# First feed-forward block with paired up tiles, and S5 set-up products on GpSimd

## The chip, the cores and the metric

The kernel runs on one core of a Trainium2 chip. The metric is the device time of one execution in microseconds, the median of the runs shown. Inside a core TensorE (PE in the profile) multiplies matrices into PSUM, VectorE (DVE) and ScalarE (ACT) work element by element, GpSimd (POOL) does so too and also issues some DMAs, and SyncE (SP) issues most DMAs. Each engine takes its instructions in the order in which they were written and waits for the others by semaphores.

## The reference, cut to what matters

The model is two blocks over 512 tokens of width 1024. The first block is a half-weighted SwiGLU feed-forward (the "first FFN", with weights w1, w3 of 1024 x 2816 and w2 of 2816 x 1024), a mixer made of an S5 state-space branch and a gated linear attention branch, and a second SwiGLU (the "second FFN") of the same shape. The second block is another mixer and a gated feed-forward with short convolutions.

```python
h = h + 0.5 * swiglu(rms_norm(h, ffn1_norm), ffn1_w1, ffn1_w3, ffn1_w2)   # (silu(x@w1) * (x@w3)) @ w2
u = rms_norm(h, mix_norm)
...                                                        # u @ w_in, S5 mixer, GLA mixer, w_out
h = h + 0.5 * swiglu(rms_norm(h, ffn2_norm), ffn2_w1, ffn2_w3, ffn2_w2)
# S5 mixer, the part that hangs on weights alone:
mag = exp(lam_re*dt); ar = mag*cos(lam_im*dt); ai = mag*sin(lam_im*dt)
bbar_re = fr*b_re - fi*b_im;  bbar_im = fr*b_im + fi*b_re  # and these times powers of (ar, ai)
```

## The kernel before

Activations lie transposed, as tiles of 128 features x 512 tokens; `KD` = 8 such tiles make the width, `NFF` = 22 make the hidden width. Every fp32 factor is split in two parts in the fp32r type, high (`wh`, `hgh`, `gh`) and low (`wl`, `hgl`, `gl`), and each product is three matmuls: high by high, high by low, low by high (`mm3`). ScalarE makes the high part by a copy and VectorE the low part by a subtraction (`wsplit`, `split_of`, `split`). For some weights (`moved=True`) the low part is made otherwise: ScalarE writes the negated high part, and a DMA issued by GpSimd adds the raw weight onto it (`dma_add`, L421); in the first FFN these are the w3 tiles.

No loop exists at run time: Python writes all operations into a `Recorder`, with an engine, a cost, a class (URGENT before MAIN before BACK) and the tiles they read and write. `Recorder.schedule` plays a planner through them with these costs, and the order that it finds on each engine is written out as the fixed instruction order. Tiles of 512 columns all come from one pool, `gen`, of 67 buffers; raw weights have 3 buffers (`raw`), split weights 4 each (`wh`, `wl`), combinations of weights 2 (`ws`). PSUM has 4 banks for the main products (`mm`) and 4 for side work (`aux`).

The first FFN: the up products of tiles 0 and 1 (`up0`) are worked out during the first loads. Tiles 2 to 21 follow one by one in `up_tile`: w1 and w3 products by `linear` (24 matmuls of 512 columns each), then the gate. The down product of tiles 0 to 15 goes through `gated`, `Pairs.put` and `down_pair`: four tiles make a part, and for two output tiles at a time `seven` computes a 2x2 block product by seven products of half width (256 tokens) in place of eight, with combinations of the weights (`ws`) and of the activations (`x1`, `x2`, `xa`, `xb`) made on VectorE. Tiles 16 to 21 go down plainly. `swiglu` calls `gated` and then does this plain rest.

The second FFN is `swiglu_pairs`: tiles 0 to 5 plainly by `up_tile`, tiles 6 to 21 two at a time by `pair8`, which forms the up product of two tiles by the same seven half-width products (7 x 4 x 3 = 84 matmuls of 256 columns for w1, and as many for w3), with combinations of the activations made once in `forms` and those of the weights in `ws`; the down products are plain, in five parts (`DOWN`), two output tiles per `linear_pair`.

`s5_prep` works out what the S5 branch needs of its weights. It is in class BACK and is planned into the first FFN's time: a chain on columns of 16 (tiles `sp`), then four blocks `b`, each with the cosines and sines (`ta`, `tt`, of 512 columns), the complex products of B and C with powers of the state matrix (elements of 128 columns, into `binr`, `bini`, `car`, `cai`, with `y1`, `y2` in an `sp` tile between), four transposes each and small matmuls on TensorE (`aux`), and spills to DRAM that GpSimd issues (`dram<-sw`, `dram<-T`). `s5_run` loads these again in the mixer.

All VectorE tensor-by-tensor operations have line L355, the scalar-tensor-tensor ones L367; all matmuls but transposes have L408.

Of the kernel before, what the change touches and what calls it, by code (L numbers as in the profile page):

```python
# [12 lines left out]
ALU = mybir.AluOpType  # L13
# [3 lines left out]
KD = D // 128  # L17
# [276 lines left out]
def body(ctx, tc, A, out):  # L294
    nc = tc.nc
# [55 lines left out]
    def dve1(o):  # L351
        return 0.068 + _size(o) / 960.0

    def tt(o, a, b, op):
        R.op("dve", dve1(o), lambda: nc.vector.tensor_tensor(out=o, in0=a, in1=b, op=op), [o], [a, b])  # L355

    def mul(o, a, b):
        tt(o, a, b, ALU.mult)

    def add(o, a, b):  # L360
        tt(o, a, b, ALU.add)
# [476 lines left out]
    UP0 = 6  # L838
    DOWN = ((0, 4), (4, 8), (8, 12), (12, 16), (16, NFF))

    def swiglu_pairs(hg, rB, h, done):
        a, jobs = [], []

        def down(p, n):
            k0, k1 = DOWN[p]
            for i, ps in enumerate(linear_pair("ffn2_w2_%d" % p, n, a[k0:k1])):
                add(h[n + i], ps, h[n + i])

        def queue():
            p = [k1 for _, k1 in DOWN].index(len(a)) if len(a) in [k1 for _, k1 in DOWN[:-1]] else None  # L850
            if p is not None:
                jobs.extend((p, n) for n in range(0, KD, 2))

        xs = forms(hg, [rB])
        for n in range(UP0):
            a.append(split(up_tile("ffn2_w1", "ffn2_w3", n, hg, rB), "g"))
            queue()
            if jobs:
                down(*jobs.pop(0))
        for i in range((NFF - UP0) // 2):  # L860
            us = pair8(A["ffn2_w1_g"][i], xs, rB)
            for u in us:
                act(u, u, AF.Silu)
            if jobs:
                down(*jobs.pop(0))
            vs = pair8(A["ffn2_w3_g"][i], xs, rB)
            for u, v in zip(us, vs):
                stt(v, v, 0.5, u, ALU.mult, ALU.mult)
                a.append(split(v, "g"))
            if jobs:  # L870
                down(*jobs.pop(0))
            queue()
        while jobs:
            down(*jobs.pop(0))
        p = len(DOWN) - 1
        for n in range(KD):
            ps = linear("ffn2_w2_%d" % p, n, a[DOWN[p][0]:])
            with cls(URGENT):
                add(h[n], ps, h[n])
                done(h[n], n)  # L880

    def swiglu(w1, w3, w2, hg, rB, h, done, up0=()):
        rest = gated(w2, lambda n: up_tile(w1, w3, n, hg, rB, up0), h)
        for n in range(KD):
            ps = linear(w2 + "_r", n, rest)
            with cls(URGENT):
                add(h[n], ps, h[n])
                done(h[n], n)
# [3 lines left out]
    with cls(BACK):  # L892
        s5_prep(locals())
    hg0, hg, st = hg, [None] * KD, []
    swiglu("ffn1_w1", "ffn1_w3", "ffn1_w2", hg0, rB, h,
           lambda t, n: norm_tile(t, Vall("mix_norm"), n, st, hg), up0)
    rB, rc = norm_end(st)
    h, hg, st = mixer1(locals())
    rB, _ = norm_end(st)
# [8 lines left out]
        norm_tile(t, fgm, n, st, hg)  # L908
        accumulate(st2, t, fg[:, n:n + 1])

    swiglu_pairs(hg0, rB, h, both)
    with cls(URGENT):
        r3 = rsqrt(mean_sq(1.0 / D, EPS, st[0]), 4)
        m2 = mean_sq(1.0 / D, 0.0, st2[0])
# [65 lines left out]
def s5_prep(env):  # L980
# [72 lines left out]
    def cmul(xr, xi, ar, ai, br, bi, t1, t2):  # L1053
# [4 lines left out]
        mul(t2, ai, br)  # L1058
        add(xi, t1, t2)

    t1, t2 = col(), col()
    P = {m: (col(), col()) for m in (1, 2, 3, 4)}
    mul(P[1][0], mag, cs)
# [35 lines left out]
    for b in range(4):  # L1099
        js = slice(4 * b, 4 * b + 4)  # L1100

        def bc(c, n):
            return c[:, js].unsqueeze(2).to_broadcast([128, 4, n])

        def spill(t):
            d = e.dtile(t.dtype)
            e.dma("pool", d, t)
            return d

        def copied(src):  # L1110
            t = lslot("sw")
            act(t if len(src.shape) == 2 else v3(t), src, AF.Copy)
            return spill(t)

        def v3(t):
            return t.rearrange("p (j c) -> p j c", j=4)


        A_, B_, n_, t_ = lslot("ta"), lslot("tb"), lslot("tn"), lslot("tt")
        io = e.Cc("iota").unsqueeze(1).to_broadcast([128, 4, 128])  # L1120
        mul(v3(A_), io, bc(ra, 128))
        mul(v3(B_), io, bc(rb, 128))
        add(n_, A_, B_)
        ts(n_, n_, INV2PI, MAGIC, ALU.mult, ALU.add)
        ts(n_, n_, MAGIC, None, ALU.subtract)
        stt(t_, n_, -C1, A_, ALU.mult, ALU.add)
        stt(t_, n_, -C23, t_, ALU.mult, ALU.add)
        add(t_, t_, B_)
        ts(t_, t_, -PI_SAFE, PI_SAFE, ALU.max, ALU.min)
        stt(A_, t_, -1.0, t_, ALU.mult, ALU.max)  # L1130
        act(t_, t_, AF.Sin)
        act(A_, A_, AF.Sin, scale=-1.0, bias=e.kbias[:, 1:2])
        d_cos, d_sin = spill(A_), spill(t_)


        B0 = lslot("b0")
        e.dma("sp", B0.rearrange("p (a j c) -> p a j c", a=4, j=4), e.A["s5bc"][:, :, js, :], after=[e.rB])
        b4 = B0.rearrange("p (a j c) -> p a j c", a=4, j=4)
        bre, bim, cre, cim = (b4[:, i] for i in range(4))
        bin_ = [lslot("binr"), lslot("bini")]  # L1140
        bv = [t.rearrange("p (j q c) -> p j q c", j=4, q=4) for t in bin_]
        y1 = x1.rearrange("p (j c) -> p j c", j=4)
        y2 = x2.rearrange("p (j c) -> p j c", j=4)
        cmul(bv[0][:, :, 3], bv[1][:, :, 3], bc(fr, 32), bc(fi, 32), bre, bim, y1, y2)
        for m in (1, 2, 3):
            cmul(bv[0][:, :, 3 - m], bv[1][:, :, 3 - m], bc(P[m][0], 32), bc(P[m][1], 32),
                 bv[0][:, :, 3], bv[1][:, :, 3], y1, y2)
        wr, wi = e.wide("car"), e.wide("cai")
        cr = wr.rearrange("p (j q c) -> p j q c", j=4, q=5)
        ci = wi.rearrange("p (j q c) -> p j q c", j=4, q=5)  # L1150
        e.vcopy(cr[:, :, 0], cre)
        ts(ci[:, :, 0], cim, -1.0, None, ALU.mult)
        for m in (1, 2, 3, 4):
            pr, pi = bc(P[m][0], 32), bc(P[m][1], 32)
            mul(y1, pr, cre)
            mul(y2, pi, cim)
            sub(cr[:, :, m], y1, y2)
            mul(y1, pr, cim)
            mul(y2, pi, cre)
            stt(ci[:, :, m], y1, -1.0, y2, ALU.mult, ALU.subtract)  # L1160
        d_cr, d_ci = (copied(t[:, :, 1:5].rearrange("p j q c -> p j (q c)")) for t in (cr, ci))

        d_bin = []
        for t in bin_:
            ps = e.auxps()
            for j in range(4):
                e.tr(ps[:, j * 128:(j + 1) * 128], t[:, j * 128:(j + 1) * 128])
            d_bin.append(copied(ps))


        ps = e.auxps()
        bb = [e.wide_u()[:, 0:512], e.wide_u()[:, 0:512]]
        for i in range(2):
            act(bb[i].rearrange("p (j q c) -> p j q c", j=4, q=4),
                bv[i][:, :, 3:4].to_broadcast([128, 4, 4, 32]), AF.Copy)
        for j in range(4):
            o = ps[:, j * 128:(j + 1) * 128]
            e.mm(o, bb[0][:, j * 128:(j + 1) * 128], wr[:, j * 160:j * 160 + 128], True, False)
            e.mm(o, bb[1][:, j * 128:(j + 1) * 128], wi[:, j * 160:j * 160 + 128], False, True)
        T = lslot("T")  # L1180
        e.zero(T, after=[ps])
        Tv = T.rearrange("p (j c) -> p j c", j=4)
        pv = ps.rearrange("p (j c) -> p j c", j=4)
        dIv = x3.rearrange("p (j c) -> p j c", j=4)
        mul(dIv, e.V("s5_d", 4 * b, 4).unsqueeze(2).to_broadcast([128, 4, 32]),
            e.Cc("i32").unsqueeze(1).to_broadcast([128, 4, 32]))
        for q in range(4):
            pr = slice(32 * q, 32 * q + 32)
            act(Tv[pr, :, 32 * q:128], pv[pr, :, 0:128 - 32 * q], AF.Copy)
            add(Tv[pr, :, 32 * q:32 * q + 32], Tv[pr, :, 32 * q:32 * q + 32], dIv[pr])  # L1190
        d_T = spill(T)
        e.s5w.append((d_bin[0], d_bin[1], d_cr, d_ci, d_T, d_cos, d_sin))
# [518 lines left out]
def arrays_of(inputs):  # L1711
    a = {k: np.asarray(v) for k, v in inputs.items()}
    r = {}
    r["x"] = np.ascontiguousarray(a["x"][0].T).reshape(8, 128, 512)
    for n in ("ffn2_w1", "ffn2_w3"):
        r[n] = _wlay(a[n][0][:, :768])
        r[n + "_g"] = _wpairs(a[n][0][:, 768:], ((0, 8),))
    for p in range(5):
        r["ffn2_w2_%d" % p] = _wlay(a["ffn2_w2"][0][512 * p:512 * p + 512 if p < 4 else None])
    for n in ("ffn1_w1", "ffn1_w3", "s5_glu_w",  # L1720
              "proj_s5", "proj_gla", "w_out", "w_in_2", "p_a_2", "p_b_2", "w_out_2", "w_up_2"):
        r[n] = _wlay(a[n][0])
    for n in ("ffn1_w2", "w_down_2"):
        r[n + "_s"] = _wpairs(a[n][0], ((0, 4), (4, 8), (8, 12), (12, 16)))
        r[n + "_r"] = _wlay(a[n][0][2048:])
    w = a["w_in"][0]
# [74 lines left out]
```

## Time and profile before

| what | value |
|---|---|
| time, median of 3 runs (lowest to highest) | 1780.22 us (1780.22 to 1780.59) |
| the profiled execution's own time | 1779.6 us |
| its span, first to last instruction | 1777.8 us |
| PE, DVE, ACT, POOL busy | 99%, 80%, 52%, 5% of the span |
| granted TensorE clock, mean | 0.997 |
| first FFN after its early tiles, first matmul of tile 2 to first of the mixer | 30.2 to 372.9 us |
| second FFN, first to last matmul | 692.7 to 1040.6 us |

The profiled execution lies 0.6 us under the median of the runs; 1.8 us of its time lie outside the span. A busy PE is not PE at its peak, since matmuls overlap and their ends are modelled: the spacing of matmul starts tells what one costs.

### The profile page before, as it was taken

The page shows a single profiled execution, that of the slowest core. Times are in us where ns is not written, and L with a number is a line of the kernel's source. Part 1 is how long each engine was busy: PE and PEld are TensorE (multiplying, and loading weights), DVE is VectorE, ACT ScalarE, POOL GpSimd, SP SyncE. Part 2 cuts the span into 40 slices and gives each one's busy share as a digit, 9 for nine tenths or more (in the row PEclk, how much of TensorE's full clock was granted, in tenths as well). Part 3 has the DMA queues.
Part 4 walks back from the last instruction along what each step waited for, and adds up shares of the span by engine and source line. Part 5 has one row for each costly group of instructions (what it writes and reads, how often), then busy time and mean ns, then how long its engine had stood idle before and what let it go on. Part 6 is the DMA issues. An engine that isn't in the chain of part 4 may idle for free. (4 is left out here: it accounts for less than half of the span.)

```text
span 1777.8 us, 25154 instructions
## 1 busy us (share of the span) xinstructions
PE 1760.8 (99%) x9514; PEld 1525.4 (86%) x9514; DVE 1422.5 (80%) x2604; ACT 929.0 (52%) x1263; POOL 96.1 (5%) x180
## 2 busy tenths in 40 slices
PE   9999999999999999999999999999999999999997
PEld 7888888878789888899999988888888888888886
DVE  8899999668799777678888889787856587887875
ACT  6444444432746533334444544999953454544443
POOL 0011111211100000000000001000000000000000
PEclk9999999999999999999999999999999999999998
DMA  8455455665313342322333334222234444444551
GB/s 247 118 151 164 141 159 169 180 222 179 104 48 107 108 142 83 107 83 96 109 105 106 97 113 165 84 95 95 81 104 142 119 119 141 121 130 135 138 142 48
DMA packets 77690, 222.17 MB, mean 125 GB/s; under 512 B 8736, under 2 KB 17728, under 8 KB 77568
## 3 DMA queue, kind: packets, MB, share of 16 engines
q1 hardware_dynamic: 64352, 175.68, 30.4%
q0 software_dynamic: 13072, 44.87, 10.5%
q8 instruction: 75, 1.23, 0.3%
q14 instruction: 47, 0.39, 0.1%
q10 hardware_dynamic: 144, 0.00, 0.0%
HBM read 182.77 MB, written 15.73 MB: 112 GB/s over the span
## 5 line engine op out<-in xcount | busy, mean ns | idle before, releaser
L408 PE MATMUL mm<-hgh,wh 128*128 128x512 f32 (+1 forms) x1440 | 539.2, 374 | 0.5 <-DVE ua L355 0.5
L408 PE MATMUL mm<-hgl,wh 128*128 128x512 f32 (+1 forms) x1440 | 539.1, 374 | 0.0
L400 ACT ACTIVATE wh<-raw 128x1024 fp32r<-128x1024 f32 (+3 forms) x315 | 304.1, 974 | 446.6 <-PE mm L408 314.2
L408 PE MATMUL mm<-hgh,wl 128*128 128x512 f32 (+1 forms) x1432 | 535.9, 374 | 0.0
L355 DVE TENSOR_TENSOR wl<-raw,wh 128x1024 fp32r<-128x1024 f32 (+3 forms) x272 | 298.9, 1100 | 43.4 <-ACT wh L400 42.5
L408 PEld LDWEIGHTS mm<-hgh,wh 128*128 128x128 f32 x1440 | 271.2, 188 | 45.2 <-DVE ua L355 0.9
L408 PEld LDWEIGHTS mm<-hgl,wh 128*128 128x128 f32 x1440 | 271.0, 188 | 44.0 <-issue 0.2
L408 PEld LDWEIGHTS mm<-hgh,wl 128*128 128x128 f32 x1432 | 270.2, 189 | 44.8 <-issue 0.2
L400 ACT ACTIVATE wh<-ws 128x1024 fp32r<-128x1024 f32 x76 | 80.6, 1061 | 134.6 <-PE mm L408 120.0
L355 DVE TENSOR_TENSOR h<-mm,h 128x512 f32<-128x512 f32 (+1 forms) x134 | 75.1, 560 | 56.2 <-PE mm L408 54.9
L408 PE MATMUL mm<-gl,wh 128*128 128x512 f32 x260 | 101.3, 390 | 0.0
L408 PE MATMUL mm<-gh,wl 128*128 128x512 f32 x260 | 101.2, 389 | 0.0
L408 PE MATMUL mm<-gh,wh 128*128 128x512 f32 x260 | 100.7, 390 | 0.0
L355 DVE TENSOR_TENSOR wl<-ws,wh 128x1024 fp32r<-128x1024 f32 x76 | 92.7, 1219 | 8.0 <-ACT wh L400 7.8
L408 PE MATMUL mm<-x1h,wl 128*128 128x256 f32 x304 | 86.1, 283 | 0.0
L408 PE MATMUL mm<-x1l,wh 128*128 128x256 f32 x304 | 86.1, 283 | 0.0
L408 PE MATMUL mm<-x1h,wh 128*128 128x256 f32 x304 | 86.0, 283 | 0.0
L408 PE MATMUL mm<-x2l,wh 128*128 128x256 f32 x304 | 85.6, 285 | 0.0
L408 PE MATMUL mm<-x2h,wl 128*128 128x256 f32 x304 | 84.2, 285 | 0.0
L408 PE MATMUL mm<-x2h,wh 128*128 128x256 f32 x304 | 84.0, 284 | 0.0
L400 ACT ACT_TABLE_LOAD x57 | 73.1, 1283 | 5.0 <-DMA yf<-dram 2.9
L367 DVE SCALAR_TENSOR_TENSOR y<-t,vec,y 128x511 f32<-128x511 f32 x88 | 65.7, 746 | 7.8 <-ACT y L400 6.9
(380 smaller groups left out, 3453.3 us busy)
## 6 DMA issues: line engine op xcount, KB each, us to landing
raw<-in_ffn_w_dram SPq DMA_DIRECT2D x68, 512.0 KB, 3.7
raw<-in_w_in_dram SPq DMA_DIRECT2D x50, 512.0 KB, 3.5
raw<-in_w_up_dram SPq DMA_DIRECT2D x44, 512.0 KB, 3.7
wl<-raw POOLq DMA_DIRECT2D x42, 512.0 KB, 4.5
raw<-in_ffn_w_g_dram SPq DMA_DIRECT2D x32, 512.0 KB, 3.8
raw<-in_ffn_w_s_dram SPq DMA_DIRECT2D x16, 512.0 KB, 4.5
raw<-in_w_out_dram SPq DMA_DIRECT2D x16, 512.0 KB, 3.5
raw<-in_w_down_s_dram SPq DMA_DIRECT2D x16, 512.0 KB, 4.8
```

What stands on the lines that cost most here:

```text
L355: R.op("dve", dve1(o), lambda: nc.vector.tensor_tensor(out=o, in0=a, in1=b, op=op), [o], [a, b])
L367: R.op("dve", dve1(o) + 0.06 * len(_aps(s)), lambda: nc.vector.scalar_tensor_tensor(out=o, in0=a, scalar=s, in1=b, op0=op0, op1=op1), [o], ...
L400: R.op("act", c, lambda: nc.scalar.activation(o, i, f, **kw), [o], _aps(i, scale, bias), table=TABLES.get(f), cls=cls, after=after)
L408: R.op("pe", c, lambda: nc.tensor.matmul(ps, a, b, start=start, stop=stop, **kw), [ps], [a, b])
```

## The change

The first FFN takes the second FFN's form. `swiglu_pairs` gets the name of the FFN (`f`) and the early tiles (`up0`) as arguments and is called for both; `swiglu` is gone, and `gated` with `seven` is left to the last feed-forward alone. So tiles 6 to 21 of the first FFN's up products go through `pair8`, all its down products become plain ones in five parts, and its w3 tiles 6 to 21 have their low parts made by VectorE. In both FFNs `forms` is called ahead of tile 2 in place of ahead of tile 0. Of `s5_prep`, the complex products of the four blocks are issued to GpSimd in place of VectorE: 24 operations for B and 20 for C in each block, on 128 columns; the four scalar-tensor-tensor operations of C in each block stay on VectorE.

```diff
+    def tt_pool(o, a, b, op):
+        R.op("pool", 0.1 + _size(o) / 480.0, lambda: nc.gpsimd.tensor_tensor(out=o, in0=a, in1=b, op=op), [o], [a, b])
...
-    def swiglu_pairs(hg, rB, h, done):
+    def swiglu_pairs(f, hg, rB, h, done, up0=()):
...
-        xs = forms(hg, [rB])
         for n in range(UP0):
-            a.append(split(up_tile("ffn2_w1", "ffn2_w3", n, hg, rB), "g"))
+            if n == 2:
+                xs = forms(hg, [rB])
+            a.append(split(up_tile(f + "_w1", f + "_w3", n, hg, rB, up0), "g"))
...
-            us = pair8(A["ffn2_w1_g"][i], xs, rB)
+            us = pair8(A[f + "_w1_g"][i], xs, rB)
...
-            vs = pair8(A["ffn2_w3_g"][i], xs, rB)
+            vs = pair8(A[f + "_w3_g"][i], xs, rB)
...
-    def swiglu(w1, w3, w2, hg, rB, h, done, up0=()):
-        rest = gated(w2, lambda n: up_tile(w1, w3, n, hg, rB, up0), h)
-        for n in range(KD):
-            ps = linear(w2 + "_r", n, rest)
-            with cls(URGENT):
-                add(h[n], ps, h[n])
-                done(h[n], n)
...
-    swiglu("ffn1_w1", "ffn1_w3", "ffn1_w2", hg0, rB, h,
-           lambda t, n: norm_tile(t, Vall("mix_norm"), n, st, hg), up0)
+    swiglu_pairs("ffn1", hg0, rB, h, lambda t, n: norm_tile(t, Vall("mix_norm"), n, st, hg), up0)
...
+    def cmul_p(xr, xi, ar, ai, br, bi, t1, t2):
+        e.tt_pool(t1, ar, br, ALU.mult)
+        e.tt_pool(t2, ai, bi, ALU.mult)
+        e.tt_pool(xr, t1, t2, ALU.subtract)
+        e.tt_pool(t1, ar, bi, ALU.mult)
+        e.tt_pool(t2, ai, br, ALU.mult)
+        e.tt_pool(xi, t1, t2, ALU.add)
...
-        cmul(bv[0][:, :, 3], bv[1][:, :, 3], bc(fr, 32), bc(fi, 32), bre, bim, y1, y2)
+        cmul_p(bv[0][:, :, 3], bv[1][:, :, 3], bc(fr, 32), bc(fi, 32), bre, bim, y1, y2)
         for m in (1, 2, 3):
-            cmul(bv[0][:, :, 3 - m], bv[1][:, :, 3 - m], bc(P[m][0], 32), bc(P[m][1], 32),
+            cmul_p(bv[0][:, :, 3 - m], bv[1][:, :, 3 - m], bc(P[m][0], 32), bc(P[m][1], 32),
                  bv[0][:, :, 3], bv[1][:, :, 3], y1, y2)
...
-            mul(y1, pr, cre)
-            mul(y2, pi, cim)
-            sub(cr[:, :, m], y1, y2)
-            mul(y1, pr, cim)
-            mul(y2, pi, cre)
+            e.tt_pool(y1, pr, cre, ALU.mult)
+            e.tt_pool(y2, pi, cim, ALU.mult)
+            e.tt_pool(cr[:, :, m], y1, y2, ALU.subtract)
+            e.tt_pool(y1, pr, cim, ALU.mult)
+            e.tt_pool(y2, pi, cre, ALU.mult)
             stt(ci[:, :, m], y1, -1.0, y2, ALU.mult, ALU.subtract)
```

The host lays out ffn1_w1, ffn1_w3 and ffn1_w2 as it did those of the second FFN.

## Rows read from the trace of the kernel before

**Rows 1.** The page, busy time of each engine over the span.
```profile
PE 1760.8 (99%) x9514; PEld 1525.4 (86%) x9514; DVE 1422.5 (80%) x2604; ACT 929.0 (52%) x1263; POOL 96.1 (5%) x180
```

**Rows 2.** Busy time by stretch: first FFN, second FFN.
```profile
core 0: us, PE busy (x) PEld busy (x) DVE busy (x) ACT busy (x) POOL busy (x), PEclk, DMA share, GB/s
30.20:372.90 342.70, 342.68 (x1872) 297.78 (x1873) 301.50 (x718) 162.92 (x227) 43.58 (x75) 1.00 0.53 156
692.70:1040.60 347.90, 347.90 (x2173) 315.64 (x2172) 282.48 (x418) 159.86 (x225) 0.00 (x0) 1.00 0.31 99
```

**Rows 3.** PE in order of time (start, us): ends of two gapless runs.
```profile
679.74 0.39 PE L408 MATMUL mm<-mgh,wh 128*128 128x512 f32 x1
...
692.66 0.39 PE L408 MATMUL mm<-hgh,wh 128*128 128x512 f32 x1
...
863.48 0.28 PE L408 MATMUL mm<-x1h,wh 128*128 128x256 f32 x1
...
866.36 0.28 PE L408 MATMUL mm<-x2h,wh 128*128 128x256 f32 x1
```

**Rows 4.** PE groups by shape in the first FFN: S5's small matmuls.
```profile
L408 PE MATMUL aux<-cai,wu 128*128 128x128 f32 x32 | 6.1, 273 | 0.0
```

**Rows 5.** Two stretches with `pair8` or half-width work, columns as Rows 2.
```profile
500.00:600.00 100.00, 100.00 (x721) 94.42 (x720) 95.14 (x199) 58.67 (x93) 1.05 (x2) 1.00 0.28 87
800.00:900.00 100.00, 100.00 (x707) 94.25 (x706) 87.18 (x127) 47.14 (x67) 0.00 (x0) 1.00 0.31 100
```

**Rows 6.** DVE groups by shape, second FFN (busy us, mean ns, idle before).
```profile
L355 DVE TENSOR_TENSOR wl<-raw,wh 128x1024 fp32r<-128x1024 f32 x44 | 53.7, 1220 | 5.4 <-ACT wh L400 5.2
...
L355 DVE TENSOR_TENSOR h<-mm,h 128x512 f32<-128x512 f32 x40 | 27.5, 687 | 13.8 <-PE mm L408 13.3
...
L355 DVE TENSOR_TENSOR ssum<-ssum,sq 128x512 f32<-128x512 f32 x13 | 8.4, 684 | 0.0
```

**Rows 7.** Busy time of what touches the `sp` tiles, first FFN.
```profile
30.20:372.90 342.70, 72.80 (x295) 0.72 (x3) 1.00 0.53 156
```

**Rows 8.** DVE groups by shape, first FFN: S5's work.
```profile
L355 DVE TENSOR_TENSOR sp<-sp,b 128x128 f32<-128x128 f32 x80 | 20.6, 286 | 1.0
...
L355 DVE TENSOR_TENSOR sp<-sp,binr 128x128 f32<-128x128 f32 x24 | 6.9, 287 | 0.3
...
L355 DVE TENSOR_TENSOR car<-sp,sp 128x128 f32<-128x128 f32 x16 | 4.6, 290 | 0.5
...
L379 DVE TENSOR_SCALAR tn<-tn 128x512 f32<-128x512 f32 x8 | 3.7, 466 | 0.0
...
L367 DVE SCALAR_TENSOR_TENSOR tt<-tn,ta 128x512 f32<-128x512 f32 x4 | 2.7, 685 | 0.0
...
L379 DVE TENSOR_SCALAR tt<-tt 128x512 f32<-128x512 f32 x4 | 1.7, 433 | 0.0
```

**Rows 9.** POOL groups by shape over the span.
```profile
L421 POOL DMA_DIRECT2D wl<-raw x42 | 36.6, 872 | 605.4 <-ACT wl L400 447.9 <-PE mm L408 97.0 <-ACT xah L400 37.2
...
L391 POOL MEMSET T<- 128x512 f32 x4 | 2.2, 538 | 0.0
...
L391 POOL MEMSET xr<- 128x4 f32 x4 | 0.5, 119 | 14.5 <-PE aux L408 14.5
...
L391 POOL MEMSET S<- 128x128 f32 x2 | 0.4, 199 | 1.1 <-ACT zs L400 1.1
```

**Rows 10.** DVE in order of time, S5's products in the first FFN.
```profile
108.08 0.28 DVE L355 TENSOR_TENSOR sp<-sp,bini 128x128 f32<-128x128 f32 x1
108.28 0.28 DVE L355 TENSOR_TENSOR sp<-sp,binr 128x128 f32<-128x128 f32 x1
108.60 0.29 DVE L355 TENSOR_TENSOR bini<-sp,sp 128x128 f32<-128x128 f32 x1
```

**Rows 11.** POOL in order of time: last S5 spill.
```profile
334.06 0.54 POOL L416 DMA_DIRECT2D dram<-T  x1 [6.56 <-issue]
```

**Rows 12.** The tile `U`: its matmuls in the mixer (ns min/median/max, first to last start).
```profile
L408 PE MATMUL aux<-U,s5w x96: 270/273/275, 401.6 to 462.7; 128*128 128x128 f32 x96
```

More of the change, by code (lines that the diff above doesn't have):

```diff
@@ L845, in down @@
             k0, k1 = DOWN[p]
-            for i, ps in enumerate(linear_pair("ffn2_w2_%d" % p, n, a[k0:k1])):
+            for i, ps in enumerate(linear_pair("%s_w2_%d" % (f, p), n, a[k0:k1])):
                 add(h[n + i], ps, h[n + i])
@@ L876, in swiglu_pairs @@
         for n in range(KD):
-            ps = linear("ffn2_w2_%d" % p, n, a[DOWN[p][0]:])
-            with cls(URGENT):
-                add(h[n], ps, h[n])
-                done(h[n], n)
-    def swiglu(w1, w3, w2, hg, rB, h, done, up0=()):
-        rest = gated(w2, lambda n: up_tile(w1, w3, n, hg, rB, up0), h)
-        for n in range(KD):
-            ps = linear(w2 + "_r", n, rest)
+            ps = linear("%s_w2_%d" % (f, p), n, a[DOWN[p][0]:])
             with cls(URGENT):
@@ L909, in both @@
         accumulate(st2, t, fg[:, n:n + 1])
-    swiglu_pairs(hg0, rB, h, both)
+    swiglu_pairs("ffn2", hg0, rB, h, both)
     with cls(URGENT):
@@ L1714, in arrays_of @@
     r["x"] = np.ascontiguousarray(a["x"][0].T).reshape(8, 128, 512)
-    for n in ("ffn2_w1", "ffn2_w3"):
+    for n in ("ffn1_w1", "ffn1_w3", "ffn2_w1", "ffn2_w3"):
         r[n] = _wlay(a[n][0][:, :768])
@@ L1718, in arrays_of @@
     for p in range(5):
-        r["ffn2_w2_%d" % p] = _wlay(a["ffn2_w2"][0][512 * p:512 * p + 512 if p < 4 else None])
-    for n in ("ffn1_w1", "ffn1_w3", "s5_glu_w",
+        for f in ("ffn1", "ffn2"):
+            r["%s_w2_%d" % (f, p)] = _wlay(a[f + "_w2"][0][512 * p:512 * p + 512 if p < 4 else None])
+    for n in ("s5_glu_w",
               "proj_s5", "proj_gla", "w_out", "w_in_2", "p_a_2", "p_b_2", "w_out_2", "w_up_2"):
         r[n] = _wlay(a[n][0])
-    for n in ("ffn1_w2", "w_down_2"):
+    for n in ("w_down_2",):
         r[n + "_s"] = _wpairs(a[n][0], ((0, 4), (4, 8), (8, 12), (12, 16)))
```

## Prediction

> **What bounds the kernel now.** I read first the page's busy times [rows 1]: PE is busy 99% of the span, DVE 80%, the rest far less. A busy share of PE says little by itself, so I went on to the spacing of matmul starts [rows 3]. Between 679.74 and 692.66 us lie 57 matmuls of 512 columns, each listed with no idle: 12.92 / 57 = 0.2267 us. Between 863.48 and 866.36 lie 24 of 256 columns: 0.1200 us. A half-width matmul thus costs 53% of a full one, not 50%.
>
> Then the two feed-forward stretches by these prices [rows 2]. The second FFN has, by the code, 816 full and 1344 half matmuls: 816 x 0.2267 + 1344 x 0.1200 = 185.0 + 161.3 = 346.3 us; twelve small ones of the norm stand among them, and the stretch lasts 347.9. The first FFN has 960 + 144 full ones (40 products up, 48 pieces of the plain rest times 3) and 672 half ones: 250.3 + 80.6 = 330.9; the stretch lasts 342.7. The 11.8 between are the 96 small matmuls and transposes of S5 [rows 4], 0.12 us each with the switches around them: 960 + 144 + 672 + 96 = 1872 is the count that the stretch shows. So PE waits for nothing that matters in either FFN: the number of matmuls sets the time, and every other engine has to keep up. DVE is the one near its limit: 301.5 of 342.7 us, 88%, in the first FFN. It can go higher without costing PE anything: in 500 to 600 us it is busy 95% while PE is full with 721 matmuls [rows 5].
>
> **The change on PE.** Up: 32 of the 40 products, 768 full matmuls, become 16 calls of `pair8`, 1344 half ones. Down: 672 half and 144 full ones become 528 full ones. Net: full -768 - 144 + 528 = -384, half +1344 - 672 = +672. In time -384 x 0.2267 + 672 x 0.1200 = -87.0 + 80.6 = -6.4 us. Both prices come from gapless runs, so this term is firm to some tenths. S5's 96 stay.
>
> **The change on DVE.** The second FFN shows what the new form asks: 282.5 us busy [rows 2]. The first needs less by the four low parts of w1 and w3 of tiles 0 and 1 (4 x 1.22), the four of w3 of tiles 2 to 5, which stay with GpSimd's adding DMA (4 x 1.22) [rows 6], and by seven of the 13 additions to sums of squares (7 x 0.68): 282.5 - 14.5 = 268. S5's work on DVE now: 72.8 us touch the `sp` tiles [rows 7]; the trigonometric part on 512 columns adds 3.7, five groups of 2.7 and 1.7, and two copies of C some 1.8 [rows 8]: 93.5. Of this the 176 moved instructions (44 in each of four blocks) are 20.6, two groups of 6.9 and three of 4.6 [rows 8]: 48.2 us, which leaves 45.3. After: 268 + 45 = 313 us in 342.7 - 6.4 = 336.3 us, 93%. That is under the 95% at which PE runs full, so I put the cost at nothing; 23 us are spare. Without the move to GpSimd it would be 361 us and DVE would be the bound.
>
> **On ACT**: 159.9 against 162.9 us [rows 2], half the time; nothing. **On DMA**: the weights' bytes are the same, and 16 of the 42 adding DMAs [rows 9] go away; the second FFN gets by with a DMA share of 0.31. Nothing.
>
> **On GpSimd.** No row shows a two-input operation there. From below: a fill of 128 columns takes 0.20 us; from above: one of 512 columns, 0.54 [rows 9]. A fill writes once for each column, the operation reads two and writes one. The fills rise by (0.538 - 0.199) / 384 = 0.88 ns a column, so three streams of 128 give 0.12 + 0.34 = 0.46 us; I take this. Then 44 x 0.46 = 20 us a block and 81 us in all (35 to 95). S5's products now run from some 90 us, and the last spill goes out at 334 us [rows 11], about 240 us for four blocks; on DVE a dependent one starts 0.32, an independent one 0.20 us after the last [rows 10]. The first use of the results is at 401.6 us [rows 12]. Even a chain longer by 40 us stays hidden. What queues behind these instructions on GpSimd: the four remaining adding DMAs (they come early, for tiles 2 to 5), the clearing of `T` and S5's spills, none of which PE waits for later on.
>
> The Trainium skill (GPSIMD Engine Reference, section 3.1) measures a two-input add of 2048 columns at 1.96 times DVE's time; times the 0.287 us of DVE here that is an estimate of 0.56 us an instruction and 99 us in all, which this chain would hide as well.
>
> **`forms` ahead of tile 2.** Its 32 DVE operations have tiles 2 to 5 and two down pairs as cover, 192 + 48 full matmuls, 54 us of PE; its own DVE work is some 18 us (per pair of tiles four of 512 columns at 0.68, four of 256 at 0.42). Nothing, in both FFNs.
>
> **The sum**: 1779.6 - 6.4 = 1773.2 us for the profiled execution. The median of the runs shown is 0.6 above it, so I forecast 1773.8 us, 0.36% faster. Within this case it is 1772 to 1777: some tenths of switching between widths on either side, and up to 3 us if DVE at 93% is late here and there. Less than 0.2%, 3.6 us, can't be told from no change.
>
> **Rival 1, slower: the two engines block each other's reads.** GpSimd now reads two SBUF tiles per instruction while DVE reads two as well. Before, GpSimd never read through its own datapath (it filled and issued DMAs), so no row shows whether both can. Suppose one waits while the other reads. About 62 of the second FFN's 282 us on DVE have an operand in PSUM (the largest group is `h<-mm,h` [rows 6]); the rest, 78% of a DVE that is busy 93%, would be held: 0.73 of what GpSimd reads. Per instruction the two read streams are 2 x 128 x 0.88 ns = 0.23 us, the whole one 0.46; halfway, 0.34: 176 x 0.34 x 0.73 = 44 us. Of these 23 are spare, and 21 reach PE: 1795 us. With 0.20 an instruction it is 26 - 23 = 3 us, 1777; with 0.54 it is 69 - 23 = 46, 1820. It decides the sign from 29 us of holding, 0.23 us an instruction. For it: DVE would have little slack, and its products stand in a fixed order. Against it: nothing in the trace, in either direction.
>
> The Trainium skill (SBUF - State Buffer, "Who interferes with whom") says just this: a VectorE instruction with two SBUF inputs contends with a GpSimd one that reads SBUF, and whichever comes second is blocked until the first has ended. By that rule the time is rival 1's; no row of before has a GpSimd read in it, so the trace neither agrees nor differs.
>
> **Rival 2, no change: DVE waits in its order.** In each block four scalar-tensor-tensor operations (`cai`) stay on DVE and read what GpSimd has just made; behind them in DVE's queue stand the low parts of weights that PE needs. The order was planned with 0.37 us an instruction. If it takes 0.54, GpSimd is late by 29 x 0.17 = 5 us at a block's first `cai` and by 0.9 us more at each further one; PE has some split weights in hand (a buffer of 1024 columns feeds 24 full matmuls, 5.4 us), so 1 to 3 us a block would get through: 4 to 10 us in all, 1778 to 1784, about 1780. Tight buffers work the same way: S5's tiles and the 16 of `forms` share the 67 of `gen`. Against it: S5 has the lowest class, so its DVE operations are placed late, in gaps.
>
> **Chances.** Forecast 0.48, rival 1 0.32, rival 2 0.20. Faster by over 0.2%: nearly all of the first and a quarter of the third, 0.51; within 0.2%: most of the third and the edges, 0.15; slower: 0.34. The range runs from 1771.5 to 1798 us: it leaves out the upper half of rival 1 and little below. The signs of the cases differ; the likeliest one's own range is 1772 to 1777.
>
> **What would show it.** In the first FFN: 720 full, 1344 half and S5's 96 matmuls, 2160 in all, in 336 us, spaced 0.2267 and 0.1200 without idle; DVE at about 313 us busy; 176 GpSimd instructions of 0.2 to 0.6 us; the last `dram<-T` before 380 us; nothing else moved but by 6.4 us earlier. Rival 1 shows in the durations: DVE operations of 128 x 1024 over 1.22 us wherever a GpSimd one overlaps, GpSimd ones far over 0.5, and PE idle on `wl`. Rival 2 shows as DVE idle ahead of `cai`, with GpSimd as the releaser. I am wrong if PE has idle time in the first FFN that was not there.

## The result, and the profile after

The changed kernel takes 1802.07 us (1801.74 to 1804.34), the kernel before 1780.22: ratio 1.0124 [1.0111, 1.0136], 22 us slower. The prediction was 1773.8, in a range up to 1798.0. The profiled execution took 1802.05 us, its span is 1800.2, its mean granted clock 0.991.

In the page's busy times, to be held against [rows 1], DVE is busy 24 us longer (the sum had 12 more, 313 for 301.5 in the first FFN), and GpSimd 115 us longer:

```profile
PE 1762.5 (98%) x9802; PEld 1539.9 (86%) x9802; DVE 1446.4 (80%) x2440; ACT 940.2 (52%) x1299; POOL 210.7 (12%) x340
```

Busy time by stretch, first FFN and second FFN, with the columns of [rows 2]:

```profile
30.20:395.10 364.90, 343.75 (x2161) 311.76 (x2162) 325.08 (x565) 176.83 (x266) 148.66 (x214) 0.97 0.37 115
715.10:1063.00 347.90, 347.90 (x2174) 315.63 (x2173) 282.60 (x419) 159.74 (x226) 0.00 (x0) 1.00 0.31 99
```

The second FFN lasts to the tenth what it did, although `forms` moved there too. The first has the 2160 matmuls that were forecast and lasts 364.9 us in place of 336.3: 22.2 us more than before, against 22.4 of the whole span. So all of the loss lies in this stretch. PE is idle there for 21 us, and the granted clock, 1.00 before, is 0.97. What PE and others waited for in it (us in all, times, longest):

```profile
POOL sp L358 <- DVE cai L370: 43.0, 12, 11.7
...
PE aux L414 <- POOL binr L358: 16.0, 3, 5.5
...
DVE cai L370 <- POOL sp L358: 2.4, 4, 1.2
```

```profile
PE mm L411 <- DVE wl L355: 4.2, 4, 1.6
```

L414 is the transpose of S5, L358 the new GpSimd product. That GpSimd waits 43.0 us for `cai`, whose inputs its next products overwrite, is no loss by itself: in a version below that wait is 51.0 us, and the stops are gone. Three stops of 5.0 to 5.5 us make up the 16.0. One of them on PE, in order of time (start, us, what, idle before):

```profile
353.40 0.39 PE L411 MATMUL mm<-gh,wh 128*128 128x512 f32 x1
359.25 0.48 PE L414 MATMUL aux<-cst,binr 128*128 128x128 f32 x1 [5.46 <-POOL binr L358]
359.37 0.78 PE L411 MATMUL mm<-gl,wh 128*128 128x512 f32 x1
359.95 0.41 PE L414 MATMUL aux<-cst,binr 128*128 128x128 f32 x1
360.01 0.78 PE L411 MATMUL mm<-gh,wl 128*128 128x512 f32 x1
...
363.43 0.39 PE L411 MATMUL mm<-gh,wh 128*128 128x512 f32 x1
```

A down product of the FFN is under way; PE's next instruction is a transpose of `binr`, planned between two matmuls of it; `binr` isn't there, so the down product stands too. When PE goes on, its instructions take about twice their time, 0.78 us for a full matmul in place of 0.39, for some 4 us. The granted clock behind each of the three stops (it stands behind the busy times, ahead of the DMA share):

```profile
204.20:209.70 5.50, 5.50 (x23) 4.95 (x24) 1.82 (x2) 2.66 (x4) 3.48 (x9) 0.51 0.29 82
280.90:286.00 5.10, 5.10 (x29) 5.10 (x30) 1.80 (x2) 3.00 (x5) 3.02 (x7) 0.62 0.17 63
359.25:363.40 4.15, 4.15 (x12) 3.20 (x13) 0.57 (x1) 1.63 (x3) 2.47 (x6) 0.52 0.75 209
```

That is mostly the 1.2 GHz level, after an idle of 5.0 to 5.5 us; reckoned as time by missing clock, it costs 5.50 x 0.49 + 5.10 x 0.38 + 4.15 x 0.48 = 6.6 us. The account at the first matmul of the mixer, with the forecast's -6.4 and the 4.2 of waiting for `wl`: -6.4 + 16.0 + 6.6 + 4.2 = +20.4 of 22.2. Why GpSimd is late stands in its groups; [rows 9] had no product among them:

```profile
L358 POOL TENSOR_TENSOR sp<-sp,b 128x128 f32<-128x128 f32 x80 | 56.7, 725 | 70.5 <-DVE cai L370 43.0 <-DVE sp L355 25.7
...
L358 POOL TENSOR_TENSOR car<-sp,sp 128x128 f32<-128x128 f32 x16 | 14.5, 904 | 1.2
L358 POOL TENSOR_TENSOR binr<-sp,sp 128x128 f32<-128x128 f32 x16 | 13.7, 857 | 1.2
```

All six groups together are 130.2 us for 176 products, 0.74 us each. The planner had counted 0.1 + 128 / 480 = 0.37, and the prediction 0.46. Of a block's 24 products for B, 21 come before its first transposes: 15.5 us in place of 7.7. Ahead of the first stop the last 20 of them run one after the other from 187.80 to 204.12 us, so no wait held them up. How long one takes goes with what DVE does. GpSimd just before the first stop and inside it, and DVE at the same times:

```profile
195.83 1.38 POOL L358 TENSOR_TENSOR sp<-sp,binr 128x128 f32<-128x128 f32 x1
197.29 1.45 POOL L358 TENSOR_TENSOR bini<-sp,sp 128x128 f32<-128x128 f32 x1
...
202.83 0.40 POOL L358 TENSOR_TENSOR sp<-sp,binr 128x128 f32<-128x128 f32 x1
203.19 0.40 POOL L358 TENSOR_TENSOR sp<-sp,bini 128x128 f32<-128x128 f32 x1
203.67 0.45 POOL L358 TENSOR_TENSOR binr<-sp,sp 128x128 f32<-128x128 f32 x1
```

```profile
195.53 1.42 DVE L355 TENSOR_TENSOR wl<-raw,wh 128x1024 fp32r<-128x1024 f32 x1
...
201.08 0.88 DVE L370 SCALAR_TENSOR_TENSOR ta<-tt 128x512 f32<-128x512 f32 x1
206.39 0.69 DVE L355 TENSOR_TENSOR h<-mm,h 128x512 f32<-128x512 f32 x1 [4.43 <-PE mm L411]
```

Beside DVE's operation of 1024 columns a product takes 1.38 us; from 201.96 us on DVE has nothing to do, and it takes 0.40 to 0.45.

DVE's operations with two operands in SBUF have grown as well, those with one in PSUM have not: `x<-mm,V` of 256 columns takes 411 ns, and [rows 6] had 1220 ns for the first of these:

```profile
L355 DVE TENSOR_TENSOR wl<-raw,wh 128x1024 fp32r<-128x1024 f32 x37 | 47.5, 1283 | 1.9 <-ACT wh L403 1.8
L355 DVE TENSOR_TENSOR wl<-ws,wh 128x1024 fp32r<-128x1024 f32 x32 | 40.2, 1256 | 0.7 <-ACT wh L403 0.6
```

So the theory was that the two engines hold each other's reads, that the products come later than the order was planned for, and that engines that take their instructions in order (PE at the transposes, DVE at `cai`) stop with all that is queued behind. It has two rivals: the time that DVE loses to held reads is itself the loss, or PE's new form costs more than its matmuls.

### The profile page after: what moved, and what is told of

The parts are those of the page before. It is cut to its first block, busy times and chain, and to the rows that moved or that the text cites. A ratio compares the mean times of both kernels' runs of the same rounds, so it can differ in the third digit from the quotient of the medians.

```text
span 1800.2 us, 25785 instructions
## 1 busy us (share of the span) xinstructions
PE 1762.5 (98%) x9802; PEld 1539.9 (86%) x9802; DVE 1446.4 (80%) x2440; ACT 940.2 (52%) x1299; POOL 210.7 (12%) x340
## 5 line engine op out<-in xcount | busy, mean ns | idle before, releaser
L411 PE MATMUL mm<-hgh,wh 128*128 128x512 f32 (+1 forms) x1376 | 492.2, 358 | 0.9 <-DVE ua L355 0.9
L411 PE MATMUL mm<-hgl,wh 128*128 128x512 f32 (+1 forms) x1376 | 492.0, 358 | 0.0
L411 PE MATMUL mm<-hgh,wl 128*128 128x512 f32 (+1 forms) x1368 | 488.7, 357 | 0.0
L411 PE MATMUL mm<-gl,wh 128*128 128x512 f32 x388 | 153.1, 394 | 0.0
L411 PE MATMUL mm<-gh,wl 128*128 128x512 f32 x388 | 152.5, 393 | 0.0
L411 PE MATMUL mm<-gh,wh 128*128 128x512 f32 x388 | 152.2, 394 | 0.0
L355 DVE TENSOR_TENSOR wl<-ws,wh 128x1024 fp32r<-128x1024 f32 x92 | 113.3, 1231 | 8.7 <-ACT wh L403 8.5
L411 PE MATMUL mm<-x1h,wh 128*128 128x256 f32 x368 | 106.0, 288 | 0.0
L411 PEld LDWEIGHTS mm<-gh,wl 128*128 128x128 f32 x388 | 73.5, 189 | 15.4 <-issue 0.4
L411 PEld LDWEIGHTS mm<-gh,wh 128*128 128x128 f32 x388 | 73.5, 189 | 14.4 <-issue 0.2
```

Source lines behind the costliest of these rows:

```text
L411: R.op("pe", c, lambda: nc.tensor.matmul(ps, a, b, start=start, stop=stop, **kw), [ps], [a, b])
```

## The experiments

Each ratio is to the kernel before on the same chip (1781.74, 1779.71 and 1780.42 us on three chips). "The plan kept" means that the instruction order of the changed kernel stands.

### The two halves of the change

Pairs alone, products left on VectorE:

```diff
-    def cmul_p(xr, xi, ar, ai, br, bi, t1, t2):
-        e.tt_pool(t1, ar, br, ALU.mult)
...
+    cmul_p = cmul
...
-            e.tt_pool(y1, pr, cre, ALU.mult)
+            mul(y1, pr, cre)
```

> The first FFN in pairs, S5's products left on VectorE. By my busy-time sum VectorE then has 361 us of work in 336: the bound, 1773.8 + 25 = 1799, some less if S5's tail moves into the mixer where VectorE is idle a third of the time (1785). If instead start-to-start spacing (0.20 us for an independent product, not 0.29) is what counts, VectorE needs only some 345 us: 1775 to 1785. Theory 1 has no GpSimd wait here; theory 2 neither.

1775.17 us, ratio 0.9969 [0.9958, 0.998]. The same kernel on another chip:

> The version with pairs alone once more (products on VectorE), for a tighter interval and beside the two others on one chip: 1771.5 to 1776.5 us, ratio 0.995 to 0.998, if the TensorE term of the sum (-6.4 us) is all there is.

1775.79 us, 0.9973 [0.9963, 0.9984]. The two ratios are 5.5 and 4.8 us, and the 6.4 of the sum, 0.9964, lies in both intervals: the term of PE holds, and DVE isn't the bound that the first expectation made of it (1799 or 1785 us). The stretches up to the mixer, and on in it:

```profile
30.20:359.90 329.70, 328.76 (x2099) 300.25 (x2099) 310.69 (x608) 163.36 (x237) 9.69 (x16) 1.00 0.37 115
...
400.00:500.00 100.00, 100.00 (x533) 85.55 (x532) 97.25 (x213) 58.91 (x76) 21.29 (x52) 1.00 0.57 186
```

The FFN ends 13.0 us earlier than in [rows 2], not 6.4, since 62 of S5's 96 small matmuls (2099 matmuls for 2161) now come later: S5's work, in the lowest class, runs on into the mixer and fills DVE to 97% there while PE stays full.

The products alone, with the first FFN of before:

```diff
-        cmul(bv[0][:, :, 3], bv[1][:, :, 3], bc(fr, 32), bc(fi, 32), bre, bim, y1, y2)
+        cmul_p(bv[0][:, :, 3], bv[1][:, :, 3], bc(fr, 32), bc(fi, 32), bre, bim, y1, y2)
...
-            mul(y1, pr, cre)
+            e.tt_pool(y1, pr, cre, ALU.mult)
```

> The kernel before with S5's products on GpSimd, its first FFN unchanged. Theory 1 (order): the planner again reckons with 0.37 us, so PE again meets transposes whose input is late, up to 5 us and some clock in each of four blocks: 1785 to 1815. Theory 2 (reads): VectorE has 253 us of work left in 343 us, so that 15 to 44 us of holding find room: 1778 to 1783.

1792.09 us, 1.0065 [1.005, 1.008]. So the products on GpSimd lose by themselves, in the FFN of before, where DVE has room: PE waits 8.1 us at the transposes, and the most frequent product takes 0.56 us, less than beside the pairs:

```profile
PE aux L414 <- POOL binr L358: 6.4, 3, 4.2
PE aux L414 <- POOL bini L358: 1.7, 2, 0.9
```

### What a product costs

A kernel of nothing but such operations: chains of 36 products of 128 columns on GpSimd, alone and beside VectorE operations of several kinds. It computes nothing of the reference.

```diff
+            for i in range(n):
+                nc.gpsimd.tensor_tensor(out=v(y1), in0=br, in1=v(src[1]), op=ALU.mult)
+                nc.gpsimd.tensor_tensor(out=v(y2), in0=br, in1=v(src[1][:, 128:]), op=ALU.mult)
+                nc.gpsimd.tensor_tensor(out=zz[:, :, i % 4], in0=v(y1), in1=v(y2), op=ALU.subtract)
...
+                    nc.vector.tensor_tensor(out=d, in0=src[0], in1=src[1], op=ALU.subtract)
```

> A kernel that computes nothing of the reference: it times the GpSimd product alone. Phases one after the other: 36 products of 128 columns with the shapes of S5's on GpSimd alone (tiles palone); 30 subtractions of 512 columns with two SBUF inputs on VectorE alone (dalone); then GpSimd's products beside VectorE operations with two SBUF inputs (pvstwo, dvspool), with one input in PSUM (pvspsum, dpsum), with one SBUF input (pvsone, done), and with two inputs of 1024 columns (pvsbig, big). If the two engines block each other's reads: 0.40 to 0.46 us alone on GpSimd, about 0.7 to 1.4 beside two-input VectorE operations, the latter raised from 0.68 to 0.8 to 1.1, and no rise beside PSUM inputs. If 0.7 us is what a product costs anyway: 0.7 in every phase and VectorE at 0.68 in all.

Groups of this kernel (busy us, mean ns of one): DVE beside GpSimd with two operands in SBUF, with one operand of 512 columns, with one in PSUM; then one GpSimd product beside operations of 1024 columns, of 512, and beside those with one operand in PSUM:

```profile
L781 DVE TENSOR_TENSOR dvspool<-src,src 128x512 f32<-128x512 f32 x40 | 32.1, 878 | 0.0
...
L785 DVE TENSOR_SCALAR done<-src 128x512 f32<-128x512 f32 x60 | 28.2, 546 | 0.0
L783 DVE TENSOR_TENSOR dpsum<-mm,src 128x512 f32<-128x512 f32 x40 | 24.0, 678 | 0.0
...
L771 POOL TENSOR_TENSOR pvsbig<-src,src 128x128 f32<-128x128 f32 x12 | 12.6, 1049 | 0.0
...
L771 POOL TENSOR_TENSOR pvstwo<-src,src 128x128 f32<-128x128 f32 x12 | 10.1, 842 | 0.0
...
L771 POOL TENSOR_TENSOR pvspsum<-src,src 128x128 f32<-128x128 f32 x12 | 4.8, 399 | 0.0
```

Undisturbed a product takes 0.40 to 0.45 us, three of a chain 1.37 us. Beside two operands in SBUF it takes 0.73 to 0.84, three 2.47 us; beside 1024 columns about 1.0. DVE's 40 operations of 512 columns take 32.1 us in place of 24.0, the time of those with one operand in PSUM: 36 products cost it 8.1 us, 0.23 each. With one operand in PSUM neither engine feels the other. So 0.46 was right for a product alone, and 0.74 is what it costs beside this DVE.

### Only the wait at the transposes taken away

The plan kept; the transposes read `B0`, which is there early, in place of the products:

```diff
-                e.tr(ps[:, j * 128:(j + 1) * 128], t[:, j * 128:(j + 1) * 128])
+                e.tr(ps[:, j * 128:(j + 1) * 128], t[:, j * 128:(j + 1) * 128], B0[:, j * 128:(j + 1) * 128])
```

> The changed kernel with its plan kept and one operand altered: the 32 transposes of binr and bini read the raw B tile (loaded long before) in place of the GpSimd products, so S5's B matrices come out as the raw ones transposed; every engine's order stays as planned. Theory 1 (order): PE no longer waits for GpSimd there; without another late consumer 1774 to 1780, and if ACT's copies of binr, or the small matmuls of car, now stand in line, some microseconds more, at most 1786. Theory 2 (reads): 1793 or above, since DVE is held as before.

1795.89 us, 1.0087 [1.0072, 1.0102], a time that the expectation had given to held reads. Only 5 us of span come back. The trace shows why: the 16 us at the transposes are gone, and the next that needs a product in order waits in their place, DVE at `cai`, and PE behind it for `wl`:

```profile
DVE cai L370 <- POOL sp L358: 16.1, 7, 5.6
```

```profile
PE mm L411 <- DVE wl L355: 11.1, 5, 5.2
```

That the transposes alone were the loss is thereby wrong.

### Both waits taken away

As the last, and `cai` reads the raw tiles of C:

```diff
-            stt(ci[:, :, m], y1, -1.0, y2, ALU.mult, ALU.subtract)
+            e.stt_as(ci[:, :, m], cre, cim, y1, y2)
```

> The changed kernel, plan kept, products and their reads on GpSimd kept; the transposes read the raw B tile and the 16 operations that make cai on VectorE read the raw C tile, so that neither PE nor VectorE stands waiting for a product (S5's matrices are wrong by that); ACT's copies still wait. Theory 1: what is left is VectorE held by reads, 0.23 us an instruction as the bare measurement gave, and ACT's waits: 1776 to 1783. Theory 2: 1790 or above.

1786.1 us, 1.0033 [1.002, 1.0045], between what the two theories had expected. The span is 1782.4: 17.8 us of the 1800.2 were stops for late products, or 16 by the ratios, since the profiled execution was the quickest of its six. The products still run and hold DVE, ACT still waits 3.8 us for one, and PE waits 6.8 us for `wl`.

### Late, but reading nothing; and neither

The plan kept; each product becomes four fills of its output (GpSimd reads nothing; B's and C's products are zeros), and in a second kernel one fill:

```diff
-        R.op("pool", 0.1 + _size(o) / 480.0, lambda: nc.gpsimd.tensor_tensor(out=o, in0=a, in1=b, op=op), [o], [a, b])
+        R.op("pool", 0.1 + _size(o) / 480.0, lambda: [nc.gpsimd.memset(o, 0.0) for _ in range(4)], [o], [a, b])
```

> The changed kernel, all orders kept, each GpSimd product replaced by four fills of the same output (S5's B and C matrices become zeros). Fills read nothing, so they can't hold VectorE, yet four take about as long as a product beside VectorE. Theory 1 (lateness in a fixed order, whatever causes it): PE again stands at the transposes; 1790 to 1802 if four fills take 0.7 us or more, in proportion less if they are quicker. Theory 2 (VectorE held by reads is the loss): under 1780.

> The same with one fill in place of each product: quicker than the 0.37 us of the plan, no reads. Both theories: GpSimd is never late and holds nobody; the PE term alone is left, 1773 to 1777. If it stays above 1785 the loss has another cause in the order itself.

Four fills, 0.82 us busy in all and about 0.95 from one product to the next, more than the 0.74 that they stand for: 1812.34 us, 1.0173 [1.0155, 1.0192], above the expected range, with the same stops, longer:

```profile
PE aux L414 <- POOL binr L358: 23.4, 3, 7.9
DVE cai L370 <- POOL sp L358: 13.0, 9, 2.7
```

DVE isn't held here: its `wl` of 1024 columns take 1219 ns, as in [rows 6]. One fill: 1776.32 us, 0.9978 [0.9968, 0.9987], without a stop of PE or DVE behind GpSimd. So lateness makes such a loss without a single read on GpSimd; in the changed kernel the reads are how the products come to be late.

Held reads have a share of their own, though. The kernel with both waits taken away and the one with one fill have the same order, on the same chip. In the first, DVE is busy 1451.1 us, in the second 1429.7, with 2440 operations in each: 21.4 us, 0.12 for each product. The first FFN lasts 347.2 us in the first and 340.2 in the second, and PE's waits for `wl` there are, in this order:

```profile
PE mm L415 <- DVE wl L355: 6.8, 5, 1.9
```

```profile
PE mm L411 <- DVE wl L355: 2.4, 3, 1.2
```

The ratios, 1.0033 and 0.9978, put 10 us between them, the spans 6.6. Most of that is held reads; ACT's 3.8 us at a late product are in it too.

### The planner told what a product costs

The cost in the recorder alone is changed, in two kernels, to 0.70 us and to 0.45, what a product takes undisturbed:

```diff
-        R.op("pool", 0.1 + _size(o) / 480.0, lambda: nc.gpsimd.tensor_tensor(out=o, in0=a, in1=b, op=op), [o], [a, b])
+        R.op("pool", 0.7, lambda: nc.gpsimd.tensor_tensor(out=o, in0=a, in1=b, op=op), [o], [a, b])
```

> The changed kernel with one constant altered: the planner is told 0.70 us for a GpSimd product in place of 0.37 (the changed kernel's trace shows a mean of 0.73). The same instructions, in another fixed order. Theory 1 (order): the loss is PE standing in its fixed order in front of S5's transposes while their input on GpSimd is late, 16 us of waits, and some 12 us at half clock behind them. Then the waits of PE on binr fall under 2 us, the granted clock in the first FFN is 1.00, and the time is 1772 to 1779. Theory 2 (reads): DVE, held by GpSimd's reads, is what PE waits for, and the transposes only stand where that shows; then it stays at 1793 or above, with the waits now on wl.

> The changed kernel, the planner told 0.45 us, what a product costs when VectorE reads nothing beside it, in place of 0.37. If the lateness comes from the two engines' reads, this is not enough and PE or VectorE still wait: 1785 to 1800. If the plan's cost was merely too low for a lone product, it comes to 1774 to 1780, as with 0.70.

With 0.70: 1779.46 us, 0.9992 [0.9982, 1.0001], half a microsecond above the expected range; with 0.45: 1793.32, 1.0069 [1.0054, 1.0084], PE still waiting 9.7 us at the transposes. With 0.70 neither PE nor DVE waits for a product (ACT does once, 2.7 us), although these still take long and DVE is held as much as in the changed kernel:

```profile
L358 POOL TENSOR_TENSOR sp<-sp,b 128x128 f32<-128x128 f32 x80 | 61.1, 780 | 80.2 <-DVE cai L370 51.0 <-DVE sp L355 25.7 <-DVE rs L370 1.7
```

```profile
L355 DVE TENSOR_TENSOR wl<-raw,wh 128x1024 fp32r<-128x1024 f32 x41 | 52.4, 1277 | 0.7 <-ACT wh L403 0.7
L355 DVE TENSOR_TENSOR wl<-ws,wh 128x1024 fp32r<-128x1024 f32 x32 | 40.2, 1258 | 0.5 <-ACT wh L403 0.4
```

The rival that held reads by themselves make the loss falls here: DVE is busy 1445.6 us over the span, for 1446.4 in the changed kernel and 1429.7 with one fill, so it is held as much, and the span is 23.7 us shorter. What holding costs hangs on the order too: up to 10 us in the one above, while here the whole distance to pairs alone is 4 us. The same cost of 0.70 in the kernel that has the products on GpSimd and the first FFN of before:

> The first FFN of the kernel before, the products on GpSimd, and the planner told 0.70 us for each product in place of 0.37. Theory (lateness against the plan costs most; the reads that hold each other cost the rest, and only where VectorE has no slack): the 6.4 us of TensorE waits behind GpSimd at the transposes go, the span falls from 1790.8 (same kernel with 0.37) to 1776 to 1780, the ratio is 0.998 to 1.002. Rival (the reads that hold each other cost most): the waits only change their place, and the ratio stays at 1.005 or more.

1783.61 us, 1.0016 [1.0007, 1.0025], for 1792.09 with 0.37: PE's stops go there too, and DVE waits 1.7 us at `cai`. The ratio is in the theory's range; the span of 1781.3 is 1.3 us above it. With a fitting cost, the products on GpSimd still give nothing: they are 4.3 us slower than on VectorE with pairs, 2.9 (by the ratio) without.

### Is VectorE the bound with pairs alone?

Pairs alone, with low parts of the down weights made by the adding DMA. These are 16, not the 20 of the expectation, since the last part of the down product doesn't go through `linear_pair`; it takes 16 x 1.22 = 19.5 us off DVE:

```diff
-            for i, ps in enumerate(linear_pair("%s_w2_%d" % (f, p), n, a[k0:k1])):
+            for i, ps in enumerate(linear_pair("%s_w2_%d" % (f, p), n, a[k0:k1], moved=f == "ffn1")):
```

> Pairs in the first FFN, products left on VectorE, and the low parts of the first FFN's down weights made by the adding DMA (20 of them, 1.22 us of VectorE each, 24 us in all). If VectorE is what presses in the first FFN of the version with pairs alone, as the prediction had it (361 of 336 us), this gives back 2 us or more against that version. If S5's work in the lowest class only slides into the mixer and costs nothing there, the two are equal within 1 us, or this one is slower by the DMAs it adds.

1778.73 us, 0.9991 [0.9982, 1.0]: 2.9 us slower than pairs alone on the same chip. PE now waits for the DMA, and for DVE more than without it:

```profile
PE mm L411 <- DMA wl<-raw: 2.7, 2, 1.6
PE mm L411 <- DVE wl L355: 2.3, 3, 1.1
```

DVE's freed time went to S5: it is busy 95.3% from 200 to 300 us with the DMAs and 96.2% without, and the mixer begins at 372.7 us for 359.9. The DMA's waits are mixed into this time; the plainer sign is the row of pairs alone above, where PE is busy 328.76 of 329.70 us. So DVE didn't set the time of that version.

The best version is the one with pairs alone, 0.3% faster than the kernel before.

## Why the prediction was wrong

**The failed step is the one "On GpSimd".** It priced 176 products at 0.46 us and then put the cost at nothing, since "the first use of the results is at 401.6 us", "even a chain longer by 40 us stays hidden" and what queues behind on GpSimd is nothing that "PE waits for later on". The first uses are the 32 transposes on PE, the 16 `cai` on DVE and copies on ACT, inside the first FFN and at fixed places of their queues. [rows 4] already shows PE at work on `cai` there, and the prediction counts S5's 96 small matmuls and transposes in that stretch; what is loaded at 401.6 us had gone through them. The first transpose and the last one in the kernel before:

```profile
110.85 0.27 PE L411 MATMUL aux<-cst,binr 128*128 128x128 f32 x1
...
309.77 0.27 PE L411 MATMUL aux<-cst,bini 128*128 128x128 f32 x1
```

Over the whole stretch the chain had room, 130 us of work in some 240; but each block has readers at a set place, and 8 us of lateness at its first transpose was too much. It cost 17.8 us of span, 16 by the ratios (both waits taken away): 16.0 us of stops at the transposes and 6.6 of low clock behind them, less some 4.5 that PE then waits elsewhere (2.6 more for `wl`, 1.9 for `gh` and `gl`). In spans, the changed kernel's 27.0 us above pairs alone are 17.8 of stops, 6.6 from there to one fill (most of it held reads), and 2.6 from one fill to pairs alone; by the ratios 16, 10 and 2.

**The price was off because of what ran beside it.** 0.46 us is what a product takes undisturbed (0.40 to 0.45 measured, 0.46 from start to start); beside DVE it was 0.74. The other estimate, 0.56, lies between the two. Planned with 0.45 the kernel still loses 0.69%.

**Rival 1, blocked reads, had the mechanism and missed the way to the time.** The engines do hold each other: the Trainium skill (SBUF - State Buffer, "Who interferes with whom") says so of a VectorE operation with two SBUF inputs and a GpSimd read, and the runs agree (0.40 to 0.84 us, no effect with an operand in PSUM). They don't bear out that the second is blocked until the first has ended: one after the other, a product and an operation of 512 columns would take 0.46 + 0.60 = 1.06 us, and a product was measured every 0.82. The loss to DVE was 0.23 us a product in the bare kernel, the point from which the rival decides the sign, and 0.12 in the FFN. By the rival's own sum, 176 x 0.23 x 0.73 = 30 us against 23 spare, PE would have lost 7 us through DVE alone, which is the size of what the first FFN loses, in the order of the changed kernel and with both waits taken away, by reads in place of fills (347.2 for 340.2 us); but with a fitting plan the same holding left the time at 1779.46. That the 1795 us of this rival lie close to the result is luck: most of the result came by another way.

**Rival 2, waits in order, had the way and looked at one queue.** It named `cai` on DVE at 4 to 10 us. In the changed kernel DVE waits 2.4 us there, because PE stops first at the transposes, which come before `cai` in each block; with the transposes out of the way, `cai` waits 16.1. Also, it left out the clock: a stop of 5 us costs about 2 us more.

**DVE as a sum.** 313 us were forecast, 325 measured (12 more, held reads and a window 28 us longer). That without the move "it would be 361 us and DVE would be the bound" was wrong: pairs alone are the fastest version. A busy sum takes for granted that all work must end inside the stretch; S5's could run on. Nor is the 95% "at which PE runs full" a line for every order, and by it only 6 us were spare, not 23: with both waits taken away DVE is busy 329.3 of 347.2 us, 95%, and PE is idle for 9.3.

**What held**: the counts (2160 matmuls, 176 products); -6.4 us on PE, measured alone as -4.8 and -5.5; nothing from `forms`, as the second FFN's unchanged 347.9 us shows; no cost on ACT. The last sign named, PE idle in the first FFN, is what the trace shows.

Left open: what the 4 us are by which the plan with 0.70 stays behind pairs alone was not taken apart. The 2.6 us between the span with one fill (1775.8) and pairs alone (1773.2) are the size of PE's 2.4 us for `wl` in the first, but the intervals of the two ratios overlap. How far the 1.8 us that the account at the mixer lacks are switches between kinds of matmul was not measured.

## What to carry to other kernels

When work moves to another engine, list every reader of its results in every queue, with its place in time: in a fixed order, a hidden chain is only hidden if each of its results comes before the first reader that has something urgent behind it. Give the planner the duration beside the neighbours that the work will have, not the one alone; here the plan made with 0.37 us was 23 us of span slower than the one made with 0.70, for products that take 0.74 or more. And before moving work off a busy engine, test whether its low-priority work can simply run on later.

## What the runs showed of the hardware

- A GpSimd product of 128 columns and a VectorE operation with both operands in SBUF slow each other in both directions: the product from 0.40-0.45 us to 0.73-0.84, DVE's operation of 512 columns from 0.60 us to 0.80 from start to start. They overlap in part, 0.82 us for a product in place of the 1.06 of one after the other.
- A VectorE operation with one SBUF operand of 512 columns (`done`) was slowed too, 546 ns for 417 without GpSimd. The Trainium skill (SBUF - State Buffer, "Who interferes with whom") names tensor-scalar operations among those that can take the shared ports; this run agrees.
- Behind stops of 5.0 to 5.5 us the granted clock was 0.51 to 0.62 for 4 to 5.5 us, so the three stops cost some 40% more than their length (6.6 us on 16.0).
